# Gated linear attention in a two-layer trunk: its 64x64 matmuls issued eight at a time

## The chip, the cores and the metric

The kernel runs on one core of a Trainium2 chip. The metric is the device time of one execution in microseconds. Of the kernel before, three runs took 2654.89, 2655.73 and 2658.55 us; the median is 2655.73 us. In what follows PE is TensorE, DVE is VectorE, ACT is ScalarE, POOL is GpSimd and SP is SyncE, which issues all the transfers.

## The reference

Two layers over 2048 tokens of width 1024. A layer normalises and modulates its input, projects it to 3600 columns, gives part of them to gated linear attention (4 heads, keys of 64, values of 128) and part to differential softmax attention (4 heads), gates both outputs, and projects them back onto the residual. The change touches the gated linear attention alone. After a short convolution, and with a learned forget gate, it computes for every chunk of 64 tokens and every head

```python
u = jnp.einsum('bnchk,bnchv->nbhkv', k_dec, v)      # 64 x 128 for each chunk and head
def step(state, inp):
    a_c, u_c = inp
    state = a_c[..., None] * state + u_c             # chunk after chunk
    return state, state
o = jnp.einsum('bnchk,nbhkv->bnchv', q, states)      # a chunk reads the state at its own end
o = rms_norm(o, g_out).reshape(B, S, GLA_WIDTH)
```

Everything is float32.

## The kernel before, in words

**Units and streams.** The tokens are cut into four units of 512 in each of the two layers, so there are eight units, one after the other. The work of a unit is written as generators, which run as six streams: the dense projections, the query and key preparation, the softmax attention, the gated linear attention, the normalisation of the next input, and the modulation vectors. The large projections are 128x128 by 512 matmuls in the fp32r type, three for each product (a high and a low part of each operand), and their PSUM tiles are called `acc` in the profile. In the first unit of each layer the weights come from their inputs and are split into the two parts by ACT and POOL; the later units reload the split weights.

**The part that changes.** The scan over a unit (`gla_gen`, L784 to L818) goes over four tiles of 128 tokens, each with two chunks. For each chunk (`par` 0 and 1) four matmuls, one for each head, compute `u` into one PSUM bank: the decayed keys `E` are 64 tokens by 64 key columns, and the moving operand is 64 tokens by 128 values of `vN` (rows `sc<-vN,E` of the profile). The chunk decides which half of the array's rows is used, and the parity of the head decides which half of its columns. Two DVE operations then make the new state `Sn` from the old one. When the tile has both states, two groups of four matmuls (`i` 0 and 1, the parity of the head) multiply the queries `qT` with them (rows `po<-Sn,qT`). Here `i` decides the half of the rows and the chunk the half of the columns. Behind each group stand an ACT square, a DVE sum (`gss`), a DVE scale and shift, a POOL power (`gw`) and a DVE multiply that writes the normalised output over `vN`; the PSUM tile of the group is held until that multiply is done. A float32 matmul appears in the profile as two weight loads and two matmuls, so that a group of four makes eight records.

**What sets the order.** The program is recorded first, as a list of operations with their dependences (`Program.record`), and then put in order by a list scheduler (`Program.order`, L188 to L275), which goes by estimated costs (`Program.cost`) and latencies. Among the operations of an engine that are ready at that time in its estimate it takes the one that was recorded first. The order on each engine is fixed before the kernel runs; on the chip each engine waits for the semaphores of its next instruction. PSUM tiles are given out in the order of recording, and the tags `sc`, `tp` and `po` share one pool of four banks (`ps_t`, L313), which the softmax attention uses too. The yields `pe(cost, wait)` in the generators say by how much a planning clock moves on and how long a stream lets the others go first; they set the order of recording.

Of the kernel before, what the change touches and what calls it, by code (L numbers as in the profile page):

```python
# [14 lines left out]
AF = mybir.ActivationFunctionType  # L15
ALU = mybir.AluOpType
AX = mybir.AxisListType
# [3 lines left out]
P = 128  # L21
# [4 lines left out]
CH = 64  # L26
EPS = 1e-6
# [90 lines left out]
class Program:  # L118
# [7 lines left out]
    def __init__(self, **engines):  # L126
        self.ops = []
        self.hist = {}
        self.engines = engines

    def queue(self, e):
# [8 lines left out]
    def record(self, e, method, args, kw):  # L140
# [15 lines left out]
            self.hist[v.buf] = keep  # L156
        self.ops.append((e, method, args, kw, deps, self.cost(e, method, args, kw, out), {v.buf: 0 for v in views}))

    @staticmethod
    def cost(e, method, args, kw, out):  # L160
        n = math.prod(out.shape[1:])
        if e == "S":
            return math.prod(out.shape) * 4 / 360.0
        if e == "T":
            if method == "transpose":
                return 110
            rate = {F32R: 2.4, BF16: 2.4, F32: 0.6}[args[2].dt]
            if rate == 0.6 and args[1].shape[1] < P:
                return max(n / rate * args[1].shape[1] / P, 78)
            return max(n / rate, 107 * args[1].shape[1] / P if rate == 2.4 else 216) + 3  # L170
        ins = [a for a in list(args[1:]) + list(kw.values()) if isinstance(a, View) and a is not kw.get("accum_out")]
        scalars = sum(math.prod(a.shape[1:]) == 1 for a in ins) if n > 1 else 0
        psum = any(a.buf.psum for a in ins)
        if method == "tensor_reduce":
            n = math.prod(ins[0].shape[1:])
        if e == "A":
            return 0.834 * n + (52 if psum else 93) + 93 * (scalars + ("accum_out" in kw))
        if e == "G":
            return 300 + 165 * n if kw.get("op") == ALU.pow else 100 + 2.2 * n
        fast = method in ("tensor_copy", "tensor_scalar") and not psum  # L180
        return (0.52 if fast else 1.042) * n + 68 + 61 * scalars
# [6 lines left out]
    def order(self):  # L188
        ops, N = self.ops, len(self.ops)
# [22 lines left out]
        todo = [i for i in range(N) if nd[i] == 0]  # L212
        table, flight = None, [-1e4] * 8
        work, win = {}, 3413
        res = []
        while len(res) < N:
            while todo:
                now, todo = sorted(todo), []
                for i in now:
                    e, bufs = ops[i][0], ops[i][6]  # L220
                    for b in bufs:
                        t = (b.pool, b.tag)
                        if b not in slot and (place[b] != nxt[t] or not slots[t]):
                            blocked[t].append(i)
                            break
                    else:
                        for b in bufs:
# [13 lines left out]
            while pend[e] and pend[e][0][0] <= t:  # L241
                heapq.heappush(avail[e], heapq.heappop(pend[e])[1])
            i = heapq.heappop(avail[e])
            if e == "S":
                free[e] = t + 475
                dma = end = max(dma, t + 1150, flight[-8] + 2000) + ops[i][5]
                flight.append(end)
            elif e == "A" and self.table(ops[i]) not in (None, table):
                table = self.table(ops[i])
                free[e] = end = t + ops[i][5] + 1283  # L250
            elif e == "T":
                w = int(t / win)
# [35 lines left out]
def trunk_kernel(ctx, tc, x, c, w_ada, b_ada, norm_g, w_in, conv_w, w_gk, b_gk, gla_norm_g,  # L288
# [33 lines left out]
    def sc():  # L322
        return ps_t.tile([P, 512], F32, tag="tp", name="sc")
# [4 lines left out]
    def po():  # L328
        return ps_t.tile([P, 512], F32, tag="tp", name="po")
# [185 lines left out]
    def pe(cost, wait=0.0):  # L515
        return ("pe", cost, wait)
# [179 lines left out]
    def gla_gen(l, u):  # L696
# [85 lines left out]
        wv = p_sm.tile([P, TT, 4], F32, tag="gw", name="gw", bufs=2)  # L782
        osb = vN
        for t in range(TT):  # L784
            Ss = []
            for par in range(2):
                cidx = 2 * t + par
                rs = slice(par * CH, par * CH + CH)
                up = sc()
                for hd in range(4):  # L790
                    hs = slice((hd % 2) * 64, (hd % 2) * 64 + 64)
                    T.matmul(up[hs, (hd // 2) * P:(hd // 2) * P + P], E[rs, t, hd * 64:hd * 64 + 64],
                             vN[rs, t, hd * P:(hd + 1) * P], start=True, stop=True)
                Sn = p_sm.tile([P, 2, P], F32, tag="S", name="Sn", bufs=4)
                for pair in range(2):
                    V.scalar_tensor_tensor(Sn[:, pair, :], Sp[:, pair, :], a_sb[:, pair, cidx:cidx + 1],
                                           up[:, pair * P:pair * P + P], op0=ALU.mult, op1=ALU.add)
                Sp = Sn
                Ss.append(Sn)
                yield pe(0.87, 0.9)  # L800
            for i in range(2):
                ops_ = po()
                hs = slice(i * 64, i * 64 + 64)
                for par in range(2):
                    c0 = (2 * t + par) * CH
                    for pair in range(2):
                        T.matmul(ops_[par * CH:par * CH + CH, pair * P:(pair + 1) * P], qT[hs, pair, c0:c0 + CH],
                                 Ss[par][hs, pair, :], start=True, stop=True)
                sq = p_t.tile([P, 256], F32, tag="sq", name="sq", bufs=2)
                A.activation(sq, ops_[:, 0:256], AF.Square)  # L810
                sl = ss[:, t, 2 * i:2 * i + 2]
                V.tensor_reduce(sl, sq.rearrange("p (a n) -> p a n", a=2), axis=AX.X, op=ALU.add)
                V.tensor_scalar(sl, sl, 1.0 / P, 4096.0 * EPS, op0=ALU.mult, op1=ALU.add)
                G.tensor_tensor(wv[:, t, 2 * i:2 * i + 2], sl, mhalf[:, 0:2], op=ALU.pow)
                V.tensor_tensor(osb[:, t, :].rearrange("p (a b n) -> p b a n", b=2, n=P)[:, i],
                                ops_[:, 0:256].rearrange("p (a n) -> p a n", n=P),
                                wv[:, t, 2 * i:2 * i + 2].unsqueeze(2).to_broadcast([P, 2, P]), op=ALU.mult)
                yield pe(0.87, 3.0)  # L818
        state["S"] = Sp
        GL["osb"] = osb  # L820
        done("scan", key)
# [367 lines left out]
```

## Time and profile before

The profiled execution took 2658.48 us, and its span, from the first to the last instruction, is 2656.8 us.

| quantity | value |
| --- | --- |
| median of three runs | 2655.73 us |
| profiled execution, and its span | 2658.48 us, 2656.8 us |
| PE busy | 2563.9 us (97%) |
| DVE, ACT, POOL busy | 1767.1, 1206.7, 626.2 us |
| mean share of the DMA engines | 52% |
| granted TensorE clock | 0.995 of full speed |

Nearly all work stands on one line, L284, where the helper issues the recorded operations, so the rows are told apart by their tiles: `sc<-vN,E` are the matmuls for `u`, `po<-Sn,qT` those of the queries, `acc` the projections. `64*64` in a matmul's row is the part of the array that it uses. A row that reads x8 holds eight records, that is four float32 matmuls. The timeline gives start, duration from the first start to the last end, engine, line, operation and tiles; the time in brackets is how long the engine had been idle, and after the arrow what ended it.

### The profile page before, as it was taken

How to read it: one execution, taken by the hardware profiler on the slowest of the kernel's cores; microseconds unless marked ns; L12 is line 12 of the kernel's file. 1: busy time of each engine (PE TensorE's matmuls, PEld its weight loads, DVE VectorE, ACT ScalarE, POOL GpSimd, SP SyncE). 2: the span in 40 equal slices, each digit the busy share in tenths (PEclk: the TensorE clock that was granted, in tenths of full speed). 3: DMA queues.
4: the chain of work that ended last, by engine and by line, in shares of the span. 5: the costliest groups of instructions: out<-in, count | busy, mean ns of one | idle time of the engine just before them, and what ended most of it. 6: DMA issues, size and time to landing. Idle time of an engine off the chain costs nothing. (4 is left out here: it accounts for less than half of the span.)

```text
span 2656.8 us, 41105 instructions
## 1 busy us (share of the span) xinstructions
PE 2563.9 (97%) x13987; PEld 2066.8 (78%) x13987; DVE 1767.1 (67%) x5104; ACT 1206.7 (45%) x2592; POOL 626.2 (24%) x852
## 2 busy tenths in 40 slices
PE   7999899999999999999999989999999999999997
PEld 4777678877888778888777767887788877888886
DVE  4778757874767837776838764667637786387764
ACT  3555524443344533444734563344614456154442
POOL 2455411131010210102144554111121111210111
PEclk9999999999999999999999999999999999999999
DMA  8676586446552455433277756453374433734242
GB/s 281 237 233 238 202 296 202 155 153 216 177 184 98 151 203 175 139 131 133 87 257 254 234 203 241 166 176 135 127 265 147 154 128 116 265 124 150 92 139 103
DMA packets 201612, 476.12 MB, mean 179 GB/s; under 512 B 20734, under 2 KB 78268, under 8 KB 201404
## 3 DMA queue, kind: packets, MB, share of 16 engines
q1 hardware_dynamic: 201404, 473.50, 52.1%
q8 instruction: 111, 1.82, 0.3%
q14 instruction: 97, 0.79, 0.1%
HBM read 362.29 MB, written 111.15 MB: 178 GB/s over the span
## 5 line engine op out<-in xcount | busy, mean ns | idle before, releaser
L284 PE MATMUL acc<-w,hhi 128*128 128x512 f32 x2560 | 842.1, 404 | 6.5 <-DMA w<-wd 2.8
L284 PEld LDWEIGHTS acc<-w,hhi 128*128 128x128 f32 x2560 | 462.3, 189 | 106.0 <-issue 13.2
L284 PE MATMUL acc<-w,hlo 128*128 128x512 f32 x1280 | 506.3, 397 | 0.0
L284 ACT ACTIVATE s<-s,mx 128x512 f32<-128x512 f32 (+15 forms) x256 | 308.1, 1204 | 339.6 <-DVE s L284 337.9
L284 PE MATMUL acc<-hhi,w 128*128 128x512 f32 x1024 | 370.5, 403 | 1.2 <-DVE z L284 0.5
L284 PE MATMUL acc<-w,oh 128*128 128x512 f32 x1024 | 333.8, 401 | 8.9 <-DVE t L284 5.0
L284 DVE TENSOR_SCALAR_CACHE_REDUCE s<-sc,mx 64x64 f32<-64x64 f32 (+5 forms) x640 | 307.4, 485 | 42.9 <-PE sc L284 24.7
L284 PEld LDWEIGHTS acc<-w,hlo 128*128 128x128 f32 x1280 | 241.2, 188 | 49.9 <-issue 2.0
L284 POOL MEMSET s<- 64x64 f32 x256 | 39.3, 155 | 1020.6 <-DVE s L284 466.2
L284 POOL TENSOR_TENSOR w<-raw,w 128x512 fp32r<-128x512 f32 x144 | 195.1, 1365 | 198.2 <-ACT w L284 152.7
L284 PEld LDWEIGHTS acc<-w,oh 128*128 128x128 f32 x1024 | 189.9, 189 | 54.4 <-DVE t L284 9.4
L284 PEld LDWEIGHTS acc<-hhi,w 128*128 128x128 f32 x1024 | 192.3, 188 | 39.3 <-issue 1.2
L284 ACT COPY aT<-tp 128x512 f32<-128x512 f32 (+2 forms) x320 | 162.7, 521 | 114.4 <-PE tp L284 110.6
L284 PE MATMUL po<-Vj,aT 128*128 128x128 f32 x1536 | 205.4, 278 | 5.1 <-ACT aT L284 4.8
L284 PE MATMUL acc<-w,ol 128*128 128x512 f32 x512 | 202.7, 400 | 1.0 <-DVE ol L284 0.7
L284 PEld LDWEIGHTS po<-Vj,aT 128*128 128x128 f32 x1536 | 191.7, 193 | 14.8 <-ACT aT L284 9.5
L284 DVE SCALAR_TENSOR_TENSOR s<-s,r 128x512 f32<-128x512 f32 (+2 forms) x320 | 200.5, 676 | 2.9
L284 DVE TENSOR_SCALAR_CACHE_REDUCE s<-sc 128x512 f32<-128x512 f32 (+4 forms) x256 | 158.5, 623 | 65.2 <-PE sc L284 61.1
L284 PE MATMUL acc<-hlo,w 128*128 128x512 f32 x512 | 201.2, 393 | 0.0
L284 DVE TENSOR_TENSOR ol<-oT,oh 128x512 fp32r<-128x512 f32 x128 | 105.6, 832 | 119.1 <-ACT oh L284 108.0
L284 PE MATMUL tp<-ident,s 128*128 128x128 f32 x1088 | 172.2, 274 | 11.8 <-DVE s L284 9.4
L284 POOL TENSOR_TENSOR rq<-qss,mhalf 128x4 f32<-128x4 f32 x128 | 129.0, 1027 | 191.4 <-DVE qss L284 191.0
(167 smaller groups left out, 4204.4 us busy)
## 6 DMA issues: line engine op xcount, KB each, us to landing
w<-wd SPq DMA_DIRECT2D x432, 512.0 KB, 3.7
wd<-w SPq DMA_DIRECT2D x144, 512.0 KB, 3.2
raw<-in_w_in_dram SPq DMA_DIRECT2D x112, 256.0 KB, 4.0
Kj<-kd SPq DMA_DIRECT2D x48, 512.0 KB, 4.9
wr<-in_w_ada_dram SPq DMA_DIRECT2D x128, 128.0 KB, 2.8
kd<-Kt SPq DMA_DIRECT2D x24, 512.0 KB, 3.0
Vj<-vd SPq DMA_DIRECT2D x48, 256.0 KB, 4.1
xt<-in_x_dram SPq DMA_DIRECT2D x16, 512.0 KB, 4.0
```

The source lines that it names most:

```text
L284: getattr(self.engines[e], method)(*[real(a) for a in args], **{k: real(v) for k, v in kw.items()})
```

## The change

The four groups of four matmuls of a tile become two groups of eight: the `u` of both chunks for all four heads, then the queries for both head parities. A new function `together` gives all eight the union of their dependences and of their PSUM tiles, and marks them as a group; the scheduler takes a burst's remaining matmuls before any other PE operation, and starts one only when all its PSUM tiles can be had at once. Within a burst the four quarters of the array are visited in turn, and each half of the rows writes a PSUM bank of its own. The scheduler's cost for such a matmul is set to 78 ns where it was 107. Behind the second burst, the scale-and-shift and the POOL power take both head parities in one operation. The yields around the bursts change too.

```diff
+    def together(self, first):
+
+        ops, last = self.ops, len(self.ops)
+        deps = {j for o in ops[first:last] for j in o[4] if j < first}
+        bufs = {b: 0 for o in ops[first:last] for b in o[6]}
+        for i in range(first, last):
+            ops[i][4].update(deps)
+            ops[i][6].update(bufs)
+            self.group[i] = last
...
             if rate == 0.6 and args[1].shape[1] < P:
-                return max(n / rate * args[1].shape[1] / P, 78)
+                return 78
...
-            i = heapq.heappop(avail[e])
+            if e == "T" and self.group.get(min(avail[e])) != burst:
+                rest = [j for j in avail[e] if j < burst and self.group.get(j) == burst]
+                if rest:
+                    avail[e].remove(min(rest))
+                    heapq.heapify(avail[e])
+                    heapq.heappush(avail[e], -min(rest))
+            i = abs(heapq.heappop(avail[e]))
+            if e == "T":
+                burst = self.group.get(i, 0)
...
         for t in range(TT):
+            ups = [sc() for _ in range(2)]
+            first = len(prog.ops)
+            for pair in range(2):
+                for x_ in (0, 1):
+                    for par in range(2):
+                        half = x_ ^ par
+                        hd, rs = 2 * pair + half, slice(par * CH, par * CH + CH)
+                        T.matmul(ups[par][half * 64:half * 64 + 64, pair * P:pair * P + P],
+                                 E[rs, t, hd * 64:hd * 64 + 64], vN[rs, t, hd * P:(hd + 1) * P], start=True, stop=True)
+            prog.together(first)
+            yield pe(0.65, 0.9)
             Ss = []
             for par in range(2):
                 cidx = 2 * t + par
-                rs = slice(par * CH, par * CH + CH)
-                up = sc()
-                for hd in range(4):
-                    hs = slice((hd % 2) * 64, (hd % 2) * 64 + 64)
-                    T.matmul(up[hs, (hd // 2) * P:(hd // 2) * P + P], E[rs, t, hd * 64:hd * 64 + 64],
-                             vN[rs, t, hd * P:(hd + 1) * P], start=True, stop=True)
...
                 Ss.append(Sn)
-                yield pe(0.87, 0.9)
+            yield pe(0, 2.0)
+            ops_ = [po() for _ in range(2)]
+            first = len(prog.ops)
+            for pair in range(2):
+                for x_ in (0, 1):
+                    for i in range(2):
+                        par = x_ ^ i
+                        hs, c0 = slice(i * 64, i * 64 + 64), (2 * t + par) * CH
+                        T.matmul(ops_[i][par * CH:par * CH + CH, pair * P:(pair + 1) * P], qT[hs, pair, c0:c0 + CH],
+                                 Ss[par][hs, pair, :], start=True, stop=True)
+            prog.together(first)
+            yield pe(0.65, 0.5)
...
+            V.tensor_scalar(ss[:, t, :], ss[:, t, :], 1.0 / P, 4096.0 * EPS, op0=ALU.mult, op1=ALU.add)
+            G.tensor_tensor(wv[:, t, :], ss[:, t, :], mhalf[:, 0:4], op=ALU.pow)
```

What this does to the order is seen best on PE. The first tile of the first unit, before: two groups for `u`, then the two for the queries, with projections (`acc`) between them.

```order
L284 MATMUL sc<-vN,E 64x128 x4
L284 MATMUL sc<-am,ones 128x256
L284 MATMUL acc<-w,hhi 128x512 x2
L284 MATMUL acc<-w,hlo 128x512
L284 MATMUL sc<-vN,E 64x128 x4
L284 MATMUL acc<-w,hhi 128x512 x2
L284 MATMUL acc<-w,hlo 128x512
L284 MATMUL acc<-w,hhi 128x512 x2
L284 MATMUL acc<-w,hlo 128x512
L284 MATMUL po<-Sn,qT 64x128 x4
L284 MATMUL acc<-w,hhi 128x512 x2
L284 MATMUL acc<-w,hlo 128x512
```

The same tile on PE in the changed kernel, from its burst for `u` to its burst of the queries (the helper's line is L305 there).

```order
L305 MATMUL sc<-vN,E 64x128 x8
L305 MATMUL sc<-am,ones 128x256
L305 MATMUL acc<-w,hhi 128x512 x2
L305 MATMUL acc<-w,hlo 128x512
L305 MATMUL acc<-w,hhi 128x512 x2
L305 MATMUL acc<-w,hlo 128x512
L305 MATMUL acc<-w,hhi 128x512 x2
L305 MATMUL acc<-w,hlo 128x512
L305 MATMUL acc<-w,hhi 128x512 x2
L305 MATMUL acc<-w,hlo 128x512
L305 MATMUL acc<-w,hhi 128x512 x2
L305 MATMUL acc<-w,hlo 128x512
```

The row that follows is `po<-Sn,qT 64x128 x8`. The second group for `u` has moved up to the first, past three projections, and the queries of both parities stand together.

In later units the groups before were also broken up, here on PE in the third tile of the fourth unit.

```order
L284 MATMUL po<-Sn,qT 64x128 x2
L284 MATMUL acc<-w,hlo 128x512
L284 MATMUL acc<-w,hhi 128x512
L284 MATMUL tp<-ident,s 128x128 x4
L284 MATMUL acc<-w,hlo 128x512
L284 MATMUL acc<-w,hhi 128x512
L284 MATMUL po<-Sn,qT 64x128
L284 MATMUL acc<-w,hhi 128x512
L284 MATMUL po<-Sn,qT 64x128
```

In the changed order there is no such piece: PE has 64 stretches of 64x64 matmuls, all of eight, where before it had 143 (119 of four matmuls, two of three, eight of two and 14 of one).

On DVE the first tile's states and its normalisation, before:

```order
L284 SCALAR_TENSOR_TENSOR Sn<-S,a_sb,sc 128x128 x2
L284 TENSOR_TENSOR gate_205<-sc,gate_205 128x256
L284 TENSOR_SCALAR am<-wr,cact 128x256
L284 SCALAR_TENSOR_TENSOR am<-wr,cact,am 128x256
L284 SCALAR_TENSOR_TENSOR Sn<-Sn,a_sb,sc 128x128 x2
L284 TENSOR_REDUCE gss<-sq 128x2
L284 TENSOR_SCALAR gss<-gss 128x2
```

And in the changed kernel:

```order
L305 SCALAR_TENSOR_TENSOR Sn<-S,a_sb,sc 128x128 x2
L305 TENSOR_TENSOR gate_205<-sc,gate_205 128x256
L305 SCALAR_TENSOR_TENSOR Sn<-Sn,a_sb,sc 128x128 x2
L305 TENSOR_SCALAR am<-wr,cact 128x256
L305 SCALAR_TENSOR_TENSOR am<-wr,cact,am 128x256
L305 SCALAR_TENSOR_TENSOR z<-th,acc 128x128 x2
L305 TENSOR_REDUCE gss<-sq 128x2 x2
L305 SCALAR_TENSOR_TENSOR am<-wr,cact,am 128x256
L305 TENSOR_SCALAR gss<-gss 128x4
```

The second state follows the first almost at once, both sums stand together, and one scale-and-shift takes four columns instead of two.

More of the change, by code (lines that the diff above doesn't have):

```diff
@@ L128, in __init__ @@
         self.hist = {}
+        self.group = {}
         self.engines = engines
@@ L214, in order @@
         work, win = {}, 3413
-        res = []
+        res, burst = [], 0
         while len(res) < N:
@@ L220, in order @@
                     e, bufs = ops[i][0], ops[i][6]
-                    for b in bufs:
+                    new = {}
+                    for b in sorted((b for b in bufs if b not in slot), key=place.get):
                         t = (b.pool, b.tag)
-                        if b not in slot and (place[b] != nxt[t] or not slots[t]):
+                        if place[b] != nxt[t] + new.get(t, 0) or len(slots[t]) <= new.get(t, 0):
                             blocked[t].append(i)
                             break
+                        new[t] = new.get(t, 0) + 1
                     else:
-                        for b in bufs:
+                        for b in sorted(bufs, key=place.get):
                             if b not in slot:
@@ L796, in gla_gen @@
                     V.scalar_tensor_tensor(Sn[:, pair, :], Sp[:, pair, :], a_sb[:, pair, cidx:cidx + 1],
-                                           up[:, pair * P:pair * P + P], op0=ALU.mult, op1=ALU.add)
+                                           ups[par][:, pair * P:pair * P + P], op0=ALU.mult, op1=ALU.add)
                 Sp = Sn
                 Ss.append(Sn)
-                yield pe(0.87, 0.9)
-            for i in range(2):
[L802 to L808, printed above, removed]
-                sq = p_t.tile([P, 256], F32, tag="sq", name="sq", bufs=2)
[L810 to L814, printed above, removed]
@@ new lines, in gla_gen @@
+            prog.together(first)
+            yield pe(0.65, 0.5)
+            for i in range(2):
+                sq = p_t.tile([P, 256], F32, tag="sq", name="sq", bufs=2)
+                A.activation(sq, ops_[i][:, 0:256], AF.Square)
+                V.tensor_reduce(ss[:, t, 2 * i:2 * i + 2], sq.rearrange("p (a n) -> p a n", a=2), axis=AX.X,
+                                op=ALU.add)
+            V.tensor_scalar(ss[:, t, :], ss[:, t, :], 1.0 / P, 4096.0 * EPS, op0=ALU.mult, op1=ALU.add)
+            G.tensor_tensor(wv[:, t, :], ss[:, t, :], mhalf[:, 0:4], op=ALU.pow)
@@ L815, in gla_gen @@
+            for i in range(2):
                 V.tensor_tensor(osb[:, t, :].rearrange("p (a b n) -> p b a n", b=2, n=P)[:, i],
-                                ops_[:, 0:256].rearrange("p (a n) -> p a n", n=P),
+                                ops_[i][:, 0:256].rearrange("p (a n) -> p a n", n=P),
                                 wv[:, t, 2 * i:2 * i + 2].unsqueeze(2).to_broadcast([P, 2, P]), op=ALU.mult)
-                yield pe(0.87, 3.0)
+            yield pe(0, 3.0)
         state["S"] = Sp
```

## The prediction

> **What bounds the kernel now.** I read the page's busy times first, then the busy time by stage, then a long unbroken piece of the chain of waits, and last the timeline of PE around single groups.
>
> ```profile
> PE 2563.9 (97%) x13987; PEld 2066.8 (78%) x13987; DVE 1767.1 (67%) x5104; ACT 1206.7 (45%) x2592; POOL 626.2 (24%) x852
> ...
> 66.40:332.10 265.70, 244.59 (x1242) 185.55 (x1241) 203.23 (x534) 143.86 (x346) 132.79 (x145) 0.99 0.67 228
> 332.10:1328.40 996.30, 983.73 (x5490) 804.64 (x5489) 680.94 (x2014) 449.87 (x931) 160.40 (x260) 1.00 0.49 167
> 1328.40:1660.50 332.10, 311.67 (x1546) 244.52 (x1546) 207.17 (x539) 154.29 (x367) 162.29 (x170) 0.98 0.69 238
> 1660.50:2590.40 929.90, 923.40 (x5137) 757.43 (x5136) 616.97 (x1846) 416.43 (x872) 146.64 (x244) 1.00 0.45 156
> ...
> 1931.52 48.36 PE acc L284 x212
> ```
>
> The rows by stage give the stretch, its length, and the busy time of PE, weight loads, DVE, ACT and POOL. PE is busy 98.7% and 99.3% of the two long stages (later units), 92.1% and 93.8% of the two short ones (first unit of each layer, where the weights are split, and DVE and POOL have their fullest hours). So PE sets the pace, wholly in six units of eight, mostly in two. The clock is granted nearly in full (0.98 to 1.00), so it can give nothing. The last row is a piece of the chain: 212 projections in a row take 48.36 us, 0.228 us each. That is the price of a PE slot in which nothing goes wrong, and the measure for the rest.
>
> "Busy" hides what this change is about: time in which the array is being emptied and refilled counts as busy, because the records of neighbours overlap. So I take the small groups' price from starts, not from busy time.
>
> ```profile
> 189.42 0.40 PE L284 MATMUL acc<-w,hlo 128*128 128x512 f32 x1
> 189.74 0.65 PE L284 MATMUL sc<-vN,E 64*64 64x128 f32 x8
> 190.33 0.73 PE L284 MATMUL acc<-w,hhi 128*128 128x512 f32 x2
> 190.90 0.39 PE L284 MATMUL acc<-w,hlo 128*128 128x512 f32 x1
> ...
> 1842.28 0.39 PE L284 MATMUL acc<-w,hlo 128*128 128x512 f32 x1
> 1842.60 0.65 PE L284 MATMUL po<-Sn,qT 64*64 64x128 f32 x4
> 1843.18 0.73 PE L284 MATMUL acc<-w,hhi 128*128 128x512 f32 x2
> 1843.75 0.39 PE L284 MATMUL acc<-w,hlo 128*128 128x512 f32 x1
> ...
> 1215.51 0.39 PE L284 MATMUL acc<-w,hhi 128*128 128x512 f32 x1
> 1215.82 0.43 PE L284 MATMUL po<-Sn,qT 64*64 64x128 f32 x2
> 1216.18 0.50 PE L284 MATMUL acc<-w,hhi 128*128 128x512 f32 x1
> 1216.61 0.43 PE L284 MATMUL po<-Sn,qT 64*64 64x128 f32 x2
> ```
>
> From 189.42 to 190.90 lie 1.48 us with three projections (3 x 0.228 = 0.68): the group of four matmuls cost 0.79 us. The second piece, with two matmuls only, costs the same: 1.47 - 0.68 = 0.79. The third, one matmul and two projections in 1.10 us, gives 1.10 - 0.46 = 0.64. The group's own pace is in the timeline cut off after the first two, four and six of its records:
>
> ```profile
> 189.74 0.33 PE L284 MATMUL sc<-vN,E 64*64 64x128 f32 x2
> 189.74 0.44 PE L284 MATMUL sc<-vN,E 64*64 64x128 f32 x4
> 189.74 0.55 PE L284 MATMUL sc<-vN,E 64*64 64x128 f32 x6
> ```
>
> Records come in pairs, and each further pair adds 0.11 us: the two column halves of the array work at the same time, on different data, while records of one half follow each other. A group of four matmuls is eight records, four in each column half, so four steps of 0.11 = 0.44 us. Two matmuls that fall in one column half (the piece at 1842.60, x4 in the same 0.65 us) also make four steps, hence the equal price. The rest, 0.79 - 0.44 = 0.35 us, does not depend on the number: it is the change from the whole array to quarters and back. The projection before is started 0.32 us ahead of the group instead of 0.23, and the two that follow need 0.57 us (190.33 to 190.90) instead of 0.46.
>
> **The change, part by part.** *Fewer changes of the array's division, and four quarters at once.* Before, PE's order holds 143 stretches: 119 of four matmuls at 0.79 us (94.0), 14 of one at 0.64 (9.0), ten of two or three, taken at 0.79 (7.9), in all 110.9 us. The changed order has 64 bursts of eight matmuls. A burst is 16 records, four for each quarter. If all four quarters work at once, it needs four steps like a group of four before, so 0.35 + 0.44 = 0.79 us, and 64 x 0.79 = 50.6 us: PE is relieved of 60.3 us. If the two row halves must take turns, there are eight steps, 0.35 + 0.88 = 1.23 us, 78.7 us in all, and 32.2 us are saved. The trace of before has no two row halves next to each other, so these are the bounds. I take the first: the column halves already share the same rows of the array and the same input partitions and still start together, whereas the row halves share neither, and the changed code gives each row half a PSUM bank of its own.
>
> The Trainium skill has a figure for this ("TensorE: Matmul & The Clock Gate", Part 3: Packing small matmuls, on the measured speedup): four row tiles side by side were measured at 3.07 times one, not 4. If two row halves lost as much, 1.53 instead of 2, the eight steps would become 5.2, a burst would cost 0.13 us more, and the sum would be 8 us worse, by estimate. No run here shows it yet.
>
> *The waits of the bursts.* The burst of `u` waits for nothing new. The burst of the queries waits for both states, where a group's first matmuls needed only the first. Its chain and what holds the PSUM banks:
>
> ```profile
> 190.45 0.61 DVE L284 SCALAR_TENSOR_TENSOR Sn<-Sn,a_sb,sc 128x128 f32<-128x128 f32 x2
> 191.92 0.66 PE L284 MATMUL po<-Sn,qT 64*64 64x128 f32 x8
> 192.69 0.39 ACT L284 ACTIVATE sq<-po 128x256 f32<-128x256 f32 x1
> 193.11 0.42 DVE L284 TENSOR_REDUCE gss<-sq 128x2 f32<-128x256 f32 x1 [2.05 <-ACT sq L284]
> 194.16 0.70 POOL L284 TENSOR_TENSOR gw<-gss,mhalf 128x2 f32<-128x2 f32 x1
> 195.18 0.41 DVE L284 TENSOR_TENSOR vN<-po,gw 128x256 f32<-128x256 f32 x1
> ```
>
> The group of 189.74 ends at 190.39, its state begins 0.06 us later and takes 0.61; both states take 1.22, so the chain is some 1.3 us. The changed order puts between the two bursts at least eight 128-wide records and three projections, 8 x 0.11 + 3 x 0.228 = 1.6 us, and in the first tile 15 projections and a small matmul. I take 0 for the wait. If DVE is full with other things and the cover is worth nothing, PE waits 1.3 us in each of 32 tiles, 42 us; behind it in PE's queue stand projections, and ACT waits for these. I keep a few us of it for the range.
>
> *The merged scale and power.*
>
> ```profile
> L284 POOL TENSOR_TENSOR rq<-qss,mhalf 128x4 f32<-128x4 f32 x128 | 129.0, 1027 | 191.4 <-DVE qss L284 191.0 <-DVE gss L284 0.4
> L284 POOL TENSOR_TENSOR gw<-gss,mhalf 128x2 f32<-128x2 f32 x64 | 45.6, 713 | 111.6 <-DVE gss L284 92.4 <-DVE r L284 15.7 <-DVE oss L284 3.1
> L284 DVE TENSOR_SCALAR gss<-gss 128x2 f32<-128x2 f32 x64 | 11.4, 178 | 0.9
> ```
>
> 64 POOL powers of 0.713 us become 32 of about 1.027 (the row of the same width), 12.7 us less; 32 DVE operations of 0.178 us go, 5.7 us. Neither engine sets the pace, so both count as 0; PE's projections hide them. What it costs is time in which PSUM is held, which is the slower rival's matter. Transfers are the same in number, and every SP instruction keeps its work; where they shift in order I count 0, with several us either way for a rearranged order of 7400 rows.
>
> *Sum.* One eighth of the 60.3 us falls in each unit. In six units PE is the bound and I count it in full: 45.2. In the first unit of each layer PE already waits for 6 to 8% of the time, for others; there I count half, 7.5 of 15.1. Together 52.8 us off the profiled execution's 2658.48 us. That execution lies 2.75 us over the median of the runs, and nothing in the sum depends on this, so the forecast is 2655.73 - 52.8 = 2603 us.
>
> **The rivals.** *The row halves take turns.* The bursts then cost 1.23 us, and PE saves 32.2 us, of which the same share (52.8/60.3) counts: 28.2 us, so 2628 us. For it: no row of before shows two row halves at once. Against it: the argument of shared inputs above. The Trainium skill ("TensorEngine Tiling (Array Packing)", Gotcha 1: PSUM Pressure) says that different row tiles cannot write one PSUM bank at the same time. This kernel writes two, so by that rule they need not take turns; no row of before bears on it.
>
> *PSUM banks, the slower one.* A bank of the queries is held from 191.92 to 195.59, 3.7 us, and two of them in a tile make 7.3 bank-us; a bank of `u` from 189.74 to 191.06, 1.3 us, 2.6 for both. After the change, both query banks wait for one chain that is longer by a square (0.39), a sum (0.42), the wider power (0.31) and a multiply (0.41): about 5.2 us each, 10.4 together; the `u` banks hold 1.3 and 1.9. So 13.6 bank-us where it was 9.9, and always two at a time of four that the softmax attention also needs. If the 3.7 bank-us are missing on the two remaining banks and PE stands still for it, that is 1.9 us a tile, 59 us in 32 tiles, and the result is 2655.7 - 52.8 + 59 = 2662 us. It decides from 1.65 us a tile (52.8/32). Against it: PE's waits for those that free banks are short now.
>
> ```profile
> PE tp L284 <- DVE s L284: 10.0, 19, 1.7
> PE po L284 <- ACT aT L284: 7.6, 11, 3.2
> ```
>
> These two, the largest of PE's waits, are 18 us in the whole span, and the order has projections to put in, which use other banks.
>
> *No change.* The whole program is ordered anew; if PE's idle time (2656.8 - 2563.9 = 93 us) grew by the 53 us saved, the time would stay at 2656. Nothing in the rows speaks for that, beyond that the scheduler's estimates now differ.
>
> **How the numbers follow.** Forecast 0.78; row halves in turn 0.12; PSUM banks 0.06; no change 0.04. All 60.3 us and a few more from the order give 2590; half of the way to the second case, for waits of the bursts or row halves that disturb each other a little, gives 2616: the forecast's own range is 2590 to 2616. The range takes in the second case with its own spread: 2589 to 2636. What a measurement of this kernel can tell from no change is about 0.2%, 5 us. Faster has the first two cases, 0.90; slower 0.06; the same 0.04.
>
> **What would show it.** In the profile after, the bursts should read x16 in about 0.65 to 0.68 us, against 1.1 if row halves take turns, and from the projection before to the third after it 1.48 us should pass, against 1.9. PE's busy time should fall by 50 to 60 us, and its idle time stay near 93. PE waits for `Sn`, or for ACT and DVE operations that read `po`, beyond some 5 us would show the cover or the banks to be missing. The forecast is wrong if PE's busy time falls by 50 us and the span does not: then another engine, or the order, is the bound.

## The result and the profile after

Five runs of the changed kernel took 2609.78 to 2617.78 us, with a median of 2615.05 us, beside 2656.93 us for the kernel before (five runs, 2654.89 to 2661.27). The ratio is 0.9839, with a 95% interval from 0.9825 to 0.9853: faster by 42 us. The forecast was 2603 us, in a range from 2589 to 2636.

The profiled execution took 2617.78 us, the slowest of the five, and its span is 2616.0 us. The page's busy times after:

```profile
PE 2513.0 (96%) x13987; PEld 2041.7 (78%) x13987; DVE 1758.4 (67%) x5072; ACT 1202.3 (46%) x2592; POOL 616.0 (24%) x820
```

The busy time by stage (stretch, its length, then busy PE, weight loads, DVE, ACT, POOL), with the stages cut at the same count of projections as those shown of before:

```profile
68.20:328.40 260.20, 236.69 (x1242) 184.17 (x1241) 201.31 (x531) 143.28 (x346) 132.70 (x141) 0.99 0.69 232
328.40:1320.20 991.80, 971.07 (x5517) 798.30 (x5515) 676.69 (x2007) 450.89 (x937) 156.44 (x250) 1.00 0.51 167
1320.20:1637.50 317.30, 300.66 (x1516) 237.89 (x1517) 207.20 (x530) 150.58 (x360) 160.23 (x164) 0.99 0.72 248
1637.50:2543.10 905.60, 897.83 (x5121) 742.89 (x5120) 609.35 (x1817) 412.94 (x868) 142.24 (x231) 1.00 0.48 160
```

PE's busy time fell by 50.9 us and the span by 40.8; PE's idle time (span less busy) rose from 92.9 to 103.0 us. A burst of the queries in the timeline of the changed kernel (start, duration, engine, line, operation and tiles, records):

```profile
192.01 0.39 PE L305 MATMUL acc<-w,hlo 128*128 128x512 f32 x1
192.33 0.67 PE L305 MATMUL po<-Sn,qT 64*64 64x128 f32 x16
192.93 0.73 PE L305 MATMUL acc<-w,hhi 128*128 128x512 f32 x2
193.50 0.39 PE L305 MATMUL acc<-w,hlo 128*128 128x512 f32 x1
```

Sixteen records take the 0.67 us that eight took before (0.65), and from 192.01 to 193.50 pass 1.49 us with three projections, 1.49 - 0.68 = 0.81 us for eight matmuls, where 0.79 us bought four. The starts within it, from the trace, in ns after the first, are 0, 7, 14, 20; 160, 167, 174, 180; 269 to 289; 379 to 399: four records at each step, so all four quarters of the array work at once.

For an account of the whole span I priced every stretch of small matmuls in the trace by starts: from the projection (or other matmul) ahead of it to the second one behind it, less the median slots of the two neighbours (a slot is the time from one start to the next). Beside PE's idle time and the time lost to the granted clock (its share below 1, over the span), the remainder should be the same for all kernels, since they do the same other work:

| kernel | stretches | priced, us | PE idle, us | lost to clock, us | span, us | remainder, us |
| --- | --- | --- | --- | --- | --- | --- |
| before | 143 | 110.5 | 92.9 | 13.8 | 2656.8 | 2440 |
| changed | 64 | 54.8 | 103.0 | 17.3 | 2616.0 | 2441 |

The remainder is equal within 1.5 us, so the account closes: 55.7 us gained on the small matmuls, 10.1 given back in idle time and 3.5 in clock (the changed kernel's profiled execution is its slowest, so the clock's part can differ from one execution to the next). (A wait inside or next to a burst counts both in its price and in the idle time, a few us.) The three parts are used below; over all kernels the remainder lies between 2436 and 2447 us, so differences of a few microseconds between two kernels are beyond this account.

PE's waits in the changed kernel, who for whom, in total, times, longest:

```profile
PE po L305 <- ACT aT L305: 12.7, 21, 3.2
PE tp L305 <- DVE s L305: 11.4, 22, 1.5
PE acc L305 <- DVE t L305: 7.1, 11, 1.3
PE sc L305 <- DVE s L305: 4.1, 10, 0.9
```

The wait of the softmax attention's `po` matmuls for `aT` was 7.6 us, that of its `sc` matmuls for `s` 1.5, that of the projections (`acc`) for `t` 5.0: most of what is new is waiting in the attention's own stream, which shares the four PSUM banks. No row names a wait of PE for `Sn`, and for the DVE multiply that frees a query bank (`vN`) PE waits 0.5 us in all, its weight loads 3 us. So a held bank hardly shows as a wait of its own; if it costs time, then by a way that these rows don't name.

### The profile page after: what moved, and what is told of

Read it like the earlier page. It is cut to its first block, busy times and chain, and to the rows that moved or that the text cites. A ratio compares the mean times of both kernels' runs of the same rounds, so it can differ in the third digit from the quotient of the medians.

```text
span 2616.0 us, 40988 instructions
## 1 busy us (share of the span) xinstructions
PE 2513.0 (96%) x13987; PEld 2041.7 (78%) x13987; DVE 1758.4 (67%) x5072; ACT 1202.3 (46%) x2592; POOL 616.0 (24%) x820
## 5 line engine op out<-in xcount | busy, mean ns | idle before, releaser
L305 PE MATMUL acc<-w,hhi 128*128 128x512 f32 x2560 | 838.9, 402 | 7.0 <-ACT ub L305 2.6
L305 PEld LDWEIGHTS acc<-w,hhi 128*128 128x128 f32 x2560 | 464.9, 189 | 100.5 <-ACT ub L305 7.7
L305 PE MATMUL acc<-w,hlo 128*128 128x512 f32 x1280 | 505.4, 396 | 0.0
L305 ACT ACTIVATE s<-s,mx 128x512 f32<-128x512 f32 (+15 forms) x256 | 308.1, 1204 | 351.0 <-DVE s L305 349.6
L305 PE MATMUL acc<-hhi,w 128*128 128x512 f32 x1024 | 370.7, 403 | 1.4 <-DVE z L305 1.2
L305 PE MATMUL acc<-w,oh 128*128 128x512 f32 x1024 | 330.8, 401 | 11.5 <-DVE t L305 7.1
L305 DVE TENSOR_SCALAR_CACHE_REDUCE s<-sc,mx 64x64 f32<-64x64 f32 (+5 forms) x640 | 307.1, 485 | 36.3 <-PE sc L305 19.1
L305 POOL MEMSET s<- 64x64 f32 x256 | 39.4, 156 | 1074.4 <-DVE s L305 527.1
L305 PEld LDWEIGHTS acc<-w,hlo 128*128 128x128 f32 x1280 | 241.4, 189 | 48.7 <-issue 1.3
L305 POOL TENSOR_TENSOR w<-raw,w 128x512 fp32r<-128x512 f32 x144 | 196.1, 1371 | 191.4 <-ACT w L305 158.9
L305 PEld LDWEIGHTS acc<-w,oh 128*128 128x128 f32 x1024 | 189.7, 190 | 58.4 <-DVE t L305 14.3
L305 PEld LDWEIGHTS acc<-hhi,w 128*128 128x128 f32 x1024 | 192.3, 188 | 39.2 <-PE tp L305 1.9
L305 PE MATMUL po<-Vj,aT 128*128 128x128 f32 x1536 | 206.1, 278 | 8.6 <-ACT aT L305 8.0
L305 ACT COPY aT<-tp 128x512 f32<-128x512 f32 (+2 forms) x320 | 162.2, 521 | 107.7 <-PE tp L305 104.4
L305 PEld LDWEIGHTS po<-Vj,aT 128*128 128x128 f32 x1536 | 191.6, 193 | 21.7 <-ACT aT L305 16.5
L305 DVE SCALAR_TENSOR_TENSOR s<-s,r 128x512 f32<-128x512 f32 (+2 forms) x320 | 200.2, 674 | 3.0
L305 PE MATMUL acc<-w,ol 128*128 128x512 f32 x512 | 201.2, 398 | 0.2
L305 PE MATMUL acc<-hlo,w 128*128 128x512 f32 x512 | 201.0, 393 | 0.0
L305 DVE TENSOR_SCALAR_CACHE_REDUCE s<-sc 128x512 f32<-128x512 f32 (+4 forms) x256 | 158.2, 622 | 57.6 <-PE sc L305 53.5
L305 DVE TENSOR_TENSOR ol<-oT,oh 128x512 fp32r<-128x512 f32 x128 | 104.7, 822 | 130.2 <-ACT oh L305 111.0
L305 PE MATMUL tp<-ident,s 128*128 128x128 f32 x1088 | 172.0, 275 | 13.5 <-DVE s L305 10.7
L305 PEld LDWEIGHTS tp<-ident,s 128*128 128x128 f32 x1088 | 130.5, 141 | 52.0 <-DVE s L305 11.9
```

Source lines behind the costliest of these rows:

```text
L305: getattr(self.engines[e], method)(*[real(a) for a in args], **{k: real(v) for k, v in kw.items()})
```

## The experiments

Two questions: is the price of a stretch what the prediction made of it, and where do the 10 us of idle time come from? Each kernel ran beside the kernel before on the same chip; the ratios are to that.

**One half of the rows at a time (e6).** Bursts of eight, as many as in the change, but each over two tiles and in one row half. Two tiles are now scanned together, which also takes a fifth state buffer (`S`), leaves one `gss` and alters the yields; this holds for e8 and f3 too.

```diff
-        for t in range(TT):
+        for t0 in range(0, TT, 2):
...
-            for pair in range(2):
-                for x_ in (0, 1):
-                    for par in range(2):
+            for par in range(2):
+                for t in (t0, t0 + 1):
+                    for pair in range(2):
+                        for half in range(2):
...
+                prog.together(first)
```

> Bursts of eight as in the change, 64 of them, but each stays in one half of the array's rows: it takes the same chunk (or the same head parity) of two neighbouring tiles. Theory: a stretch costs 0.35 us for the change of division plus 0.11 us for each step of its busiest quarter. Each quarter that is used now holds four matmuls, eight steps, so 1.23 us a burst, 78.7 us in all where the changed kernel's bursts take about 54.8 us by their starts: 24 us slower than the changed kernel, near 2639 us. Rival (only the number of stretches counts, not how many quarters work at once): 0.79 us a burst and 2615 us.

Measured: 2639.9 us (0.9931, 0.9911 to 0.9952). A burst in its timeline:

```profile
188.65 0.40 PE L305 MATMUL acc<-w,hlo 128*128 128x512 f32 x1
188.98 1.09 PE L305 MATMUL sc<-vN,E 64*64 64x128 f32 x16
190.00 0.73 PE L305 MATMUL acc<-w,hhi 128*128 128x512 f32 x2
190.57 0.39 PE L305 MATMUL acc<-w,hlo 128*128 128x512 f32 x1
```

1.92 us with three projections leave 1.24 us a burst, and all 64 cost 78.7 us. PE's idle time is 102.0 us, that of the change. So 24 us of the change's 56 come from the row halves working at once, the rest from fewer changes of division, and the theory's price (1.23 us) holds to a hundredth of a microsecond.

**Two tiles in one burst (e8).** 32 bursts of sixteen matmuls on the same two banks, of which the second tile uses the other half:

```diff
-        for t in range(TT):
+        for t0 in range(0, TT, 2):
             ups = [sc() for _ in range(2)]
...
+            for t in (t0, t0 + 1):
...
+                            o0 = (t - t0) * 256 + pair * P
...
```

> Two tiles in one burst: 32 bursts of 16 matmuls over all four quarters instead of 64 of eight, on the same two PSUM banks, whose second half is used for the second tile. Theory: eight steps, 0.35 + 0.88 = 1.23 us a burst, 39.4 us in all, 15 us less than the changed kernel: near 2600 us, with PE's idle time as in the changed kernel (103 us). Rival (the idle time that the change brought, 10 us, comes from the two banks that a burst holds at a time): they are now held for about twice as long, PE's idle time grows by 10 us or more, and the time is 2610 us or above.

Measured: 2616.7 us (0.9848, 0.9828 to 0.9868). A burst in its timeline:

```profile
193.01 0.39 PE L305 MATMUL acc<-w,hlo 128*128 128x512 f32 x1
193.33 1.10 PE L305 MATMUL po<-Sn,qT 64*64 64x128 f32 x32
194.37 0.74 PE L305 MATMUL acc<-w,hhi 128*128 128x512 f32 x2
194.95 0.40 PE L305 MATMUL acc<-w,hlo 128*128 128x512 f32 x1
```

The burst's price is as the theory has it: 1.94 - 0.68 = 1.26 us here, 1.24 in the median, 40.3 us in all, 14.5 less than in the change. But the time is the change's. Idle time rose by 3.6 us to 106.6 (less than the rival's 10), 24 us are lost to the clock where it was 17, and the span is 1.5 us shorter. The theory is wrong about the time, and the rival names the right time without its cause: of the 14.5 us, 3.6 go in idle time, 6.8 in clock, 1.5 are left as gain, and the other 2.6 the account doesn't place. The rival's premise is off as well: a query bank is held for 9.2 us in the median where it was 6.6, but half as often, so for less time in all. The attention's wait is the largest row of PE's waits.

```profile
PE po L305 <- ACT aT L305: 19.8, 20, 3.2
```

**Row halves one after the other (e5).** The order inside a burst alone:

```diff
-                for x_ in (0, 1):
-                    for par in range(2):
-                        half = x_ ^ par
+            for par in range(2):
+                for pair in range(2):
+                    for half in range(2):
```

(and the same for the queries.)

> The changed kernel with another order inside a burst: all four matmuls of the first half of the rows, then all four of the second half, instead of one quarter after the other. Theory (PE starts the matmul of a free quarter ahead of earlier ones that wait for a busy quarter): a burst still costs 0.79 us and the time stays at 2615 us within 8 us. Rival (matmuls start in the order written, so a quarter that comes late waits): the halves work one after the other, 1.23 us a burst, 28 us slower, 2640 us.

Measured: 2621.29 us (0.9865, 0.9845 to 0.9885). A burst in its timeline:

```profile
191.62 0.39 PE L305 MATMUL acc<-w,hlo 128*128 128x512 f32 x1
191.94 0.68 PE L305 MATMUL po<-Sn,qT 64*64 64x128 f32 x16
192.55 0.73 PE L305 MATMUL acc<-w,hhi 128*128 128x512 f32 x2
193.13 0.39 PE L305 MATMUL acc<-w,hlo 128*128 128x512 f32 x1
```

The burst still takes 0.68 us. Its first four starts are 0, 7, 27 and 34 ns: the second row half, which stands four matmuls later in the program, starts 27 ns after the first, ahead of records that stand before it and wait for their quarter (these start at 160 ns and later). The careful visiting of the quarters in turn isn't needed; 54.8 us is the same total, and the 6 us between the medians are within the expected 8, and the intervals of the two ratios overlap.

**Without the marking (e3).** The scheduler may break bursts up:

```diff
-            prog.together(first)
```

(twice.)

> The changed kernel without the marking of a burst: the matmuls are recorded in the same order, but the scheduler may put others between them and start them one by one. In its order the 64x64 matmuls form about 90 stretches of one to eight instead of 64. Theory (each stretch costs 0.35 us beside its steps): about 10 us slower than the changed kernel, near 2625 us. Rival (holding back a burst until both banks are free costs PE more idle time than it saves): 2610 us or less.

Measured: 2629.08 us (0.9892, 0.9877 to 0.9908), with 87 stretches priced at 72.2 us, 17.4 more than the change, and idle time of 103.4 us. The theory holds; the time is 14 us longer than the change's where it gave about 10. And a burst that may begin without its second bank doesn't give the idle time back.

**Does a new order alone move the time? (e1, e2, e9).** The first takes the change's new cost back, the second gives it to the kernel before, the third alters three planning yields of the change.

```diff
-                return 78
+                return max(n / rate * args[1].shape[1] / P, 78)
```

> The changed kernel with the scheduler's old estimate of 107 ns for a small matmul instead of 78. The bursts stay 64 of eight; only the order of everything changes a little. Theory: within 8 us of 2615 us, and what differs is idle time of PE, not the bursts. Rival (the new estimate is part of the gain, since it is nearer to a burst's 0.79 us): 10 us slower or more.

> The kernel before with the new estimate of 78 ns alone; about 145 stretches of small matmuls as before. Theory: within 8 us of 2656 us; it shows how far a new order alone moves the time. Rival (the estimate is part of the gain): 10 us faster or more.

> The changed kernel with other numbers in three planning yields around the bursts (0.8 for 0.65 twice, 1.4 for 2.0): the same work and the same 64 bursts in a slightly different order. Theory: PE's idle time moves by up to 10 us either way and the time with it, 2605 to 2625 us. Rival (the idle time belongs to the bursts): it stays at 103 us within 3 us, and so does the time.

Measured: e1 2620.92 us (0.9866, 0.9852 to 0.9881), e2 2658.82 us (1.0009, 1.0000 to 1.0019), e9 2623.81 us (0.9879, 0.9864 to 0.9894). PE's idle time is 104.1, 93.8 and 105.1 us: with bursts 102 to 106 us in six orders (the change, e1, e3, e5, e6, e9), without them 93 and 94 in two. The scatter of an order is about 2 us of idle time either way (one profiled execution of each); the 10 us are not scatter. That part of my theory fell with these three: in e9 the rival is right about the idle time, though not about the time, which is 9 us longer. The new cost is not a gain by itself (e2); whether it is worth the 6 us by which e1 is slower, I can't separate from the order. All three kernels with the change's bursts in another order (e1, e5, e9; the bursts cost 54.5 to 55.2 us in each) take 6 to 9 us more than the change, of which idle time is 1 to 3; the interval of e9 lies clear of the change's, the other two touch it. So the change's own order is in part luck: the bursts bring some 33 to 42 us, as the order falls.

**The query banks given back early (e7).**

```diff
-                A.activation(sq, ops_[i][:, 0:256], AF.Square)
+                oc = osb[:, t, :].rearrange("p (a b n) -> p b a n", b=2, n=P)[:, i]
+                A.copy(oc, ops_[i][:, 0:256].rearrange("p (a n) -> p a n", n=P))
+                A.activation(sq.rearrange("p (a n) -> p a n", n=P), oc, AF.Square)
...
-                                ops_[i][:, 0:256].rearrange("p (a n) -> p a n", n=P),
+                                osb[:, t, :].rearrange("p (a b n) -> p b a n", b=2, n=P)[:, i],
```

> The changed kernel, with the query results copied out of PSUM by ACT as soon as the burst is done (64 copies of 128x256, about 0.4 us each, into the tile that takes the output anyway); square and multiply then read the copy, so that the two banks are free some 4 us earlier. Theory (the 10 us of idle time that PE gained are the ordinary scatter of a new order, and waits that PE's saved time had covered): within 8 us of the changed kernel's 2615 us. Rival (they come from the banks that a burst holds): PE's idle time falls by about 10 us and the time to 2605 us or less.

Measured: 2611.95 us (0.9832, 0.9815 to 0.9849). From the first matmul of a burst to the last read of its banks pass 2.9 us in the median, where it is 6.6 in the change. The page's busy times, of a span of 2607.8 us:

```profile
PE 2509.8 (96%) x13987; PEld 2036.7 (78%) x13987; DVE 1761.4 (68%) x5072; ACT 1223.1 (47%) x2656; POOL 618.7 (24%) x820
```

Idle time is 98.0 us, 5 us less than the change and outside the scatter; 8 us are lost to the clock instead of 17. Half of the rival's 10 us: held query banks are part of the cause. The time is the theory's (within 8 us), and the ratio doesn't differ from the change's beyond the intervals.

**The banks held longer (f4).**

```diff
+            for _ in range(4):
+                G.tensor_tensor(wv[:, t, :], wv[:, t, :], ones[:, 0:4], op=ALU.pow)
```

> The changed kernel with the suspected cost made larger: four more POOL powers (with exponent 1) stand in the chain of each tile, so that both query banks are held about 4 us longer in each of the 32 tiles. The bursts stay 64 of eight. Theory (held banks make PE idle): as the early release took about 5 us of idle time away, this adds about as much or more, 108 us or above, and 2620 us or more. Rival (the banks do not matter): idle time 102 to 106 us and 2615 us within 5 us.

Measured: 2675.29 us (1.0065, 1.0050 to 1.0080), slower than the kernel before. The banks are held 12.8 us in the median. The page's busy times, of a span of 2673.2 us:

```profile
PE 2544.8 (95%) x13987; PEld 2056.6 (77%) x13987; DVE 1760.6 (66%) x5072; ACT 1204.0 (45%) x2592; POOL 744.9 (28%) x948
```

The longest of PE's waits:

```profile
PE po L305 <- ACT aT L305: 18.8, 28, 3.2
PE sc L305 <- DVE s L305: 16.2, 25, 1.9
PE tp L305 <- DVE s L305: 15.0, 23, 1.9
```

Idle time is 128.4 us (25 more), the bursts' price 64.0 (9 more, waits), and 45 us are lost to the clock where it was 17, with a mean granted clock of 0.983. POOL, which got 129 us more work, is busy only 28% of the time, and the three longest of PE's waits, all grown, are those of the attention's `po`, `sc` and `tp`. DVE doesn't stand behind the longer chain: it waits 8.0 us for `gw` where it was 5.6. But it waits 63.6 us for two other POOL powers (`rq`, `wq`) where it was 41.4, so that a part of the loss may come through POOL's queue and not through the banks; the two were not separated. With this reserve it is the prediction's slower rival, made real by a longer chain.

**The joint end without bursts (f1).** The kernel before, with both query banks behind one chain:

```diff
+            ops_ = []
             for i in range(2):
-                ops_ = po()
+                ops_.append(po())
...
+            V.tensor_scalar(ss[:, t, :], ss[:, t, :], 1.0 / P, 4096.0 * EPS, op0=ALU.mult, op1=ALU.add)
+            G.tensor_tensor(wv[:, t, :], ss[:, t, :], mhalf[:, 0:4], op=ALU.pow)
```

> The kernel before with four groups of four as they were, but with the change's joint end: both query banks wait for one chain of two squares, two sums, one scale, one power of four columns and two multiplies. In its order there are about 140 stretches of small matmuls, so these cost 110 us as before. Theory (PE's 10 us of new idle time come in good part from query banks that are held together and longer): PE's idle time 98 to 103 us where it was 93, and 2662 us. Rival (the idle time belongs to the bursts, or to PE being ahead): idle time 93 us and 2657 us.

Measured: 2663.45 us (1.0023, 1.0013 to 1.0033), with 140 stretches at 108.4 us. The page's busy times, of a span of 2661.5 us:

```profile
PE 2564.3 (96%) x13987; PEld 2067.5 (78%) x13987; DVE 1765.0 (66%) x5072; ACT 1204.7 (45%) x2592; POOL 616.1 (23%) x820
```

The longest of PE's waits:

```profile
PE po L284 <- ACT aT L284: 14.5, 15, 3.2
PE acc L284 <- DVE t L284: 10.3, 10, 3.2
```

2661.5 less 2564.3 is 97.2 us of idle time, 4.3 more than before: without one burst, the joint end alone costs 6.7 us. Its two query banks are held for 8.0 and 5.9 us in the median, about as long together as in the change (6.3 and 6.6). The attention waits 6.9 us more for `aT` than before, and the projections 5.3 us more for `t`.

**Bursts for u alone (f2).** The queries as before, with their own chains:

```diff
-            yield pe(0, 2.0)
-            ops_ = [po() for _ in range(2)]
+            yield pe(0, 0.9)
+            for i in range(2):
+                ops_ = po()
...
```

> The changed kernel with bursts for u alone; the queries go as before, each head parity with its own groups and its own chain. In its order 32 stretches of eight and 82 of one to four. By the prices of the two traces 32 x 0.80 + 54 x 0.79 + 19 x 0.62 + 9 x 0.78 = 87 us for the small matmuls. Theory (the idle time comes from the query banks): PE's idle time is near 93 to 96 us, and the time is 2440 (all else) + 87 + 95 + 15 (clock) = 2637 us. Rival (it comes from the bursts): idle time 98 us or more.

Measured: 2646.27 us (0.9955, 0.9939 to 0.9972), with 114 stretches at 89.2 us (2 us over the sum). Idle time is 100.3 us (2643.8 less 2543.5). The theory that the query banks alone cause it falls: bursts of `u`, which also take two banks at a time, bring 7 us with the query side as it was. The two parts (4.3 from f1, 7.4 from f2) make 11.7 us where the change has 10.1; with a scatter of 2 us in each they may well add up. The time is 9 us over the theory's 2637.

**Both ideas together (f3).** e8 with the copies of e7, all four behind the burst:

```diff
+            for i in range(2):
+                for t in (t0, t0 + 1):
+                    o1 = (t - t0) * 256
+                    oc = osb[:, t, :].rearrange("p (a b n) -> p b a n", b=2, n=P)[:, i]
+                    A.copy(oc, ops_[i][:, o1:o1 + 256].rearrange("p (a n) -> p a n", n=P))
...
```

> The 32 bursts of 16 over two tiles, with the query results copied out of PSUM by ACT right behind the burst. Theory: 32 x 1.24 = 40 us for the bursts, PE's idle time 98 to 100 us as with the early release in the changed kernel, 10 to 18 us lost to the clock: 2590 to 2600 us, faster than every version so far. Rival (with longer bursts the idle time is set by something other than the banks): idle time 106 us as with two tiles alone, and 2612 us or more.

Measured: 2624.06 us (0.9870, 0.9856 to 0.9885), slower than either. The bursts cost 44.5 us, and the banks are held for only 2.4 us in the median, yet PE's idle time is 114.2 us. The page's busy times, of a span of 2621.2 us:

```profile
PE 2507.0 (96%) x13987; PEld 2048.4 (78%) x13987; DVE 1762.7 (67%) x5072; ACT 1219.6 (47%) x2656; POOL 616.0 (24%) x820
```

Three of PE's waits:

```profile
PE po L305 <- ACT aT L305: 18.4, 18, 3.2
PE sc L305 <- DVE Kt L305: 7.5, 10, 2.1
PE sc L305 <- DVE xss L305: 6.7, 2, 3.5
```

A miss for the theory, and against the banks as the only cause. The `aT` that PE waits for most is written by ACT, which now does four copies in a row there; that this delays it was only argued. What makes PE idle with two-tile bursts stays open.

## Why the prediction was right, and where it was off

**The price of a stretch: right.** A fixed 0.35 us plus 0.11 us for each step of the busiest quarter gave 0.79 us for a burst and 1.23 if row halves took turns. Measured were 0.80 us in the change, 1.22 with one row half, 1.24 with sixteen matmuls (medians over all stretches). The total fell by 55.7 us against 60.3; about 3 of the 4.6 us lie in five bursts next to which PE waited, so that 64 of them cost 54.8 us instead of 50.6.

**Four quarters at once: right.** The argument from shared inputs held; e6 shows what the other bound would have cost, at 2640 us (forecast for it: 2628). The estimate from the Trainium skill ("TensorE: Matmul & The Clock Gate", Part 3: Packing small matmuls), 0.13 us more a burst, did not come true: two row halves lost 0.01 us, not a quarter of their gain. The Trainium skill's rule in "TensorEngine Tiling (Array Packing)", Gotcha 1: PSUM Pressure, isn't contradicted: all kernels here give each row half its own bank.

**The waits of the bursts and the merged operations: right for the time, wrong for PSUM.** PE has no row of waiting for `Sn`; POOL lost 10.2 us of work and DVE 8.7, without effect. But the sum put the joint chain's hold of the banks at nothing and left it to the slower rival, and that was wrong: f1 puts the joint end at 4.3 us of idle time and 6.7 us of time. The prediction estimated the hold of a query bank at 5.2 us after 3.7 us; over all tiles it is 6.6 us after 4.5 in the median, where the shortest of the same chain takes 4.0: the rest is waiting behind other work. The sign that the prediction named for missing banks, waits of PE for what reads `po`, didn't come (0.5 us); the banks tell in other rows.

**The conversion into time: the failed step.** The sum let 52.8 of the 60.3 us count, and put the loss of 7.5 us in the first unit of each layer, since PE waits there already. The span fell by 40.8 us (the medians by 41.9), and the loss lies elsewhere. By stage, idle time was 21.1, 12.6, 20.4 and 6.5 us, and is 23.5, 20.7, 16.6 and 7.8: the two first units together were idle 1.4 us less than before, and the later units of the first layer 8.2 us more. Their stage of 996.3 us became only 4.5 us shorter, while the last stage lost 24.3. (Part of this is work moved between stages: the second holds 27 more PE records than before, the third 30 fewer. The start and the end of the span, outside the four stages, became 8.3 us longer together, with 2.1 us of idle time.) In place of a PE held up in the first units stands a new cost that the change brought: 10 us of idle time, most of it waits in the stream of the attention, which shares four PSUM banks with bursts that take two. The prediction had held banks as its slower rival, with 0.06 and a price of 59 us; it was not an alternative to the forecast but a part of it, at about 5 of the 10 us for the query banks (e7, f1). f4 shows it larger: 12.8 us of hold and 2675 us. That the time still fell within the forecast's own range of 2590 to 2616 us is in part the luck of the order: e1, e5 and e9, with the same bursts, lie above it, at 2621 to 2624.

**What stays open.** The query banks are part of the 10 us (f1 and e7: about 5), and bursts of `u` bring 7 on their own (f2), which within the scatter is the whole. Whether the bursts of `u` cost this through their banks or through the place of the attention in the new order was not separated; f3 shows idle time that neither explains.

## What to carry to other kernels

Price short matmuls of another array division by their stretches, from the start of the neighbour ahead to the second start behind, and not by busy time or by their number: here 0.35 us for each stretch and 0.11 us for each step, whether two or four quarters work. Join them into long stretches over all quarters, with a PSUM bank for each row half (as in all kernels here; one bank for both was not tried), but count in what a longer chain behind them does to those who share the banks and the engines: four more small operations behind the burst turned a gain of 42 us into a loss of 19. When a kernel is ordered by a planner, run two or three neutral variants of its estimates first, so that a few microseconds of idle time can be told from scatter.

## What the runs showed of the hardware that was not expected

PE starts matmuls out of program order when their quarter of the array is free: 27 ns after the first, ahead of earlier records that start at 160 ns or later (e5). The granted clock isn't constant at a PE that is 96% busy: in the traces it stood at half in stretches of 3.4 us or a few times that (up to 17 us, in f4), in which a projection's slot took 0.427 us instead of 0.227, and the time lost in this way ranged from 8 us (e7, mean clock 0.997) to 45 us (f4, 0.983). Idle time goes ahead of it: in the changed kernel each of the eight such stretches begins behind 3.4 us in which PE was idle for 62% or more, and over the fourteen traces 125 of 127 begin behind 30% or more, which only 3% of all pieces of that length have. Not every such piece is followed by one, and the total isn't in proportion (e3 10.5 us with 103 us of idle time, e8 24 with 107). In the change's five runs the clock goes with the spread: 2609.78 us came with a mean of 0.996, 2617.78 with 0.993.
